# An encoder block on one core: TensorE's instructions held in the kernel's own order, the pieces of five stages and of the last gate rearranged

## The chip, the cores and the metric

The kernel runs on one core of a Trainium2 chip. The metric is the time of one execution of the whole program in device microseconds; the figure for the kernel before is the median of three runs. One further execution was recorded by the hardware profiler; all rows of the trace are of that one.

## What is computed

One layer of a bidirectional encoder, 256 tokens by 2048 features, all in float32:

```python
h = rms_norm(x, attn_norm)
qa, ka, va, qb, kb, vb, ga, gb = split(h @ w_in)
ya = windowed_gqa(qa, ka, va, ...)          # 8 heads, banded
yb = dilated_attention(qb, kb, vb, ...)     # 12 heads in 3 groups
merged = sigmoid(ga) * (ya @ w_branch_a) + sigmoid(gb) * (yb @ w_branch_b)
x = x + merged @ w_out
hf = rms_norm(x, ffn_norm)
g = dwconv_centred(hf @ w_ffn_gate, conv_w, conv_b)
x = x + (gelu(g) * (hf @ w_ffn_up)) @ w_ffn_down
gate_p = sigmoid(rms_norm(x, ple_norm) @ w_ple_gate)
x = x + gate_p * (p @ w_ple_proj)
return rms_norm(x, final_norm)
```

Nearly all of the work is the product of 256 rows with some 340 MB of weights, each of which is read once.

## The kernel before, in words

**Products in two halves.** A float32 operand is split into a high part that TensorE's fast float32 format holds exactly and a low rest. A product is then three fast matmuls: high by high, high by low, low by high (`thirds`, lines 466 to 468 for the high and low of both operands). For every weight block of 128x128 ScalarE makes the high part (L357, into `wh` or `vh`) and VectorE the low one (L358, into `wl` or `vl`). These go into a store of 56 blocks, 40 in the tiles `w*` and 16 in `v*`, which is used as a ring: `drop` gives blocks back when the kernel has written down their last matmul, and calls `pump`, which at once writes down the production of the next units as long as they fit (`produce`). So at each place of the program the weights of the next two pieces or so are written down already, and VectorE, which takes its instructions in one fixed order, has them ahead of what the kernel writes later.

**Pieces by eight and by seven.** The weight stream is cut into pieces. Within a stage that multiplies 128-token rows by two column groups of 512 (`quads`, `quad_stage`), a piece covers two chunks of 128 features. Kind "s" makes the 2x2 block product with eight `thirds`, which is 24 matmuls; kinds "Z" and "Y" make it after Winograd with seven, which is 21, from sums of the activations (`combos`, made by `combine` and `sums_of`) and sums of the weights. Part of the sums of the weights is made in DRAM by adding DMAs from GpSimd's queue (`sum_ahead`), part by VectorE in `sum_of_weights` (L336). A piece by seven puts 28 blocks through the store and a piece by eight 16. The strings `GATES`, `OUTS`, `DOWN` and `ALT` say piece by piece which kind it is.

**Stages.** In order of the program: A (projections and attention); for j = 0 to 3 a gate stage Bj, then `ba`j and `bb`j (the two branch products of kind "w", 24 matmuls a piece); D0 and D1 (the output projection, 8 pieces each); E0 (gate and up of the first half of the MLP: each `product` is 16 matmuls 128x512 and then 16 of 128x256, lines 409 and 416; the first four products run jointly); F00 and F01 (the down projection, 11 pieces each); E1, F10, F11 likewise for the second half; pp0 and pp1 (the projection of p, one "s" piece each); then the last gate: G0 (8 pieces, two column groups, kinds by `ALT`), G2 and G3 (4 pieces each, kind "w", one column group each); and the final norm.

**The end of a quad stage.** The seven sums lie in the PSUM banks M1, M7, M5, M6, M2, M3, M4, and the fourth result in P22; pieces by eight write M2, M3, M4 and P22 alone. In the last piece, which is by eight, `row_sums` first combines M1, M6, M7, M5 (L938 to L942) and then, after every second of its eight `thirds`, calls `end(t, n)` for row half t and column group n. In D and F this is `residual`'s `finish`: L1059 adds the bank to the residual rows `xr`, and for n = 1 L1061 adds the combined sums over all 1024 columns of that row half. `end(1, 1)` has slot 8: it is written down after the last `thirds`, after the blocks of the last piece were given back and after the units that then fit the store were written down.

**Turns.** The next product needs the new rows turned round: `turn_back` takes a pair of feature chunks and makes four TensorE transpositions (L987) in the order (chunk 0, half 0), (chunk 0, half 1), (chunk 1, half 0), (chunk 1, half 1) into one PSUM bank, which ScalarE and VectorE then read out (L571 and L572, or L990 and L991). `rows_pair` turns `xr` into `hf` (before E0) or `pl` (before the last gate), `merged_pair` turns the gated rows into `merged`. Where these stand in the program is set by `at((stage, piece, slot), ...)`: they are written down before that slot's `thirds`; in E0 the place is the chunk number k of the joint products, and 16 matmuls are written at a time.

**What sets the order on the engines.** The framework's scheduler takes the program and its own estimate of times and fixes the order of each engine's instructions: of those that it thinks ready it takes the one that stands first in the program. An instruction that would wait is overtaken, on TensorE too. Once fixed, each engine runs its list in order.

Of the kernel before, what the change touches and what calls it, by code (L numbers as in the profile page):

```python
# [20 lines left out]
D = 2048  # L21
KC = D // P
# [71 lines left out]
WIDE = 2 * T  # L94
_JOBS = _plan()
NA = len(_JOBS)
ALT = "ZsZsZsZs"
GATES = ("sssssYYs", "YsYYsYYs", "YsYYsYYs", "YsYYsYYs")
OUTS = "ZsZZsZZs"
DOWN = ("YYsYsYsYsYs", "ZsZZsZsZsZs")  # L100


def _ffn(half):
# [10 lines left out]
def _pieces():  # L114

    pieces, stages = [], {}

    def blocks(stage, items):
        stages[stage] = range(len(pieces), len(pieces) + len(items) // PIECE)
        for i in range(0, len(items), PIECE):  # L120
            pieces.append(("f", items[i:i + PIECE]))

    def quads(stage, n0, n1, pattern, k0=0):
        stages[stage] = range(len(pieces), len(pieces) + len(pattern))
        for i, c in enumerate(pattern):
            a, b = k0 + 2 * i, k0 + 2 * i + 1
            pieces.append((c, [(n1, a), (n1, b), (n0, a), (n0, b)] if c == "Z" else
                           [(n1, a), (n0, a), (n1, b), (n0, b)] if c == "Y" else
                           [(n0, a), (n1, a), (n1, b), (n0, b)]))

    def wide(stage, n, chunks):
        stages[stage] = range(len(pieces), len(pieces) + chunks // 4)
        for k in range(0, chunks, 4):
            pieces.append(("w", [(n, k + i) for i in range(4)]))

    a = [("w_in", k, j[2]) for k in range(KC) for j in _JOBS[:FIRST]]
    for _, _, n in _JOBS[FIRST:]:
        a += [("w_in", k, c) for k in range(KC) for c in (n if isinstance(n, tuple) else (n,))]
    blocks("A", a)
    for j in range(4):  # L140
        quads("B%d" % j, ("w_in", GA * P + j * WIDE), ("w_in", GB * P + j * WIDE), GATES[j])
        wide("ba%d" % j, ("w_branch_a", j * WIDE), QH)
        wide("bb%d" % j, ("w_branch_b", j * WIDE), HG)
    for s in range(2):
        quads("D%d" % s, ("w_out", 2 * s * WIDE), ("w_out", (2 * s + 1) * WIDE), OUTS)
    for half in range(2):
        names = {"g": "w_ffn_gate", "u": "w_ffn_up"}
        jobs = [(names[kind], f) for kind, f in _ffn(half)]
        joint = 0 if half else JOINT
        e = [(name, k, f) for k in range(KC) for name, f in jobs[:joint]]  # L150
        e += [(name, k, f) for name, f in jobs[joint:] for k in range(KC)]
        blocks("E%d" % half, e)
        for s in range(2):
            quads("F%d%d" % (half, s), ("w_ffn_down", 2 * s * WIDE), ("w_ffn_down", (2 * s + 1) * WIDE),
                  DOWN[half], half * FHALF)
    for s in range(2):
        stages["pp%d" % s] = [len(pieces)]
        n0, n1 = ("w_ple_proj", 2 * s * WIDE), ("w_ple_proj", (2 * s + 1) * WIDE)
        pieces.append(("s", [(n0, 0), (n1, 0), (n1, 1), (n0, 1)]))
    quads("G0", ("w_ple_gate", 0), ("w_ple_gate", WIDE), ALT)  # L160
    for s in (2, 3):
        wide("G%d" % s, ("w_ple_gate", s * WIDE), KC)
    return pieces, stages


# [31 lines left out]
def _encoder(ctx: ExitStack, tc, xt, pt, xrow, cols, gainrow, table, onehot, mask, ident_in, wts, out):  # L197
# [50 lines left out]

    made, taken, raws, left_of = {}, {}, {}, {}
    state = {"unit": 0, "at": 0, "early": True, "load": 0}  # L250
    store, free = {}, deque()
    rawt = wpool.tile([P, RAW * P], F32, name="raw")
    rawfree = deque(range(RAW))
    loads = []
# [2 lines left out]
    def extend(which, pool):  # L257

        store[which] = [pool.tile([P, STORE[which] * P], FR, name=which + half) for half in ("h", "l")]
        free.extend((which, b) for b in range(STORE[which]))  # L260

    extend("w", wpool)

# [116 lines left out]

    def drop(u, n=None):
        n = n or len(taken[u])
        free.extend(taken[u].popleft() for _ in range(n))
        made[u][1] += n
        if not taken[u]:
            del made[u], taken[u]
        pump()
# [82 lines left out]
    def part(m, t):  # L470
        return [m[:, c + t * P:c + (t + 1) * P] for c in (0, T)]

    def quad_stage(stage, moving, combos=None, tags=("M2", "M3", "M4", "P22")):
# [24 lines left out]
        for i, p in enumerate(pieces):  # L498
            kind = _PIECES[p][0]
            us = _UNITS_OF[p]  # L500
            if (stage, i) not in ends:
                a, b = moving(2 * i), moving(2 * i + 1)
            if kind == "s":
                final = i == len(pieces) - 1
                for g in range(8):
                    run_due(stage, i, g)
                    t, n, c = (g // 4, g // 2 % 2, g % 2) if final else (g // 2 % 2, g % 2, g // 4)
                    w = cut(us[c], n if c == 0 else 1 - n)
                    put(tags[2 * t + n], part((a, b)[c], t), w)
                    if not final and g % 4 == 3:  # L510
                        drop(us[c])
                if final:
                    drop(us[0])
                    drop(us[1])
            else:
                s = combos(i)
                sums = [(s[:, 0, e], s[:, 1, e]) for e in range(4)]
                m1, m2, m4 = (part(a, 0), part(b, 0), part(b, 1)) if (stage, i) not in ends else ends[stage, i]
                if kind == "Z":
                    todo = (("M6", sums[1], 0, 0), ("M3", sums[3], 0, 1), ("M1", m1, 1, 0), ("M2", m2, 1, 1),  # L520
                            ("M7", sums[2], 2, 0), ("M4", m4, 2, 1), ("M5", sums[0], 2, 2))
                else:
                    todo = (("M6", sums[1], 0, 0), ("M1", m1, 0, 1), ("M3", sums[3], 1, 0), ("M2", m2, 1, 1),
                            ("M7", sums[2], 2, 0), ("M5", sums[0], 2, 1), ("M4", m4, 2, 2))
                for g, (name, stationary, u, c) in enumerate(todo):
                    run_due(stage, i, g)
                    put(name, stationary, cut(us[u], c))
                    drop(us[u], 4)
# [84 lines left out]
    def spread_sums(pieces, slots):  # L613

        last = len(slots) - 10
        for e, p in enumerate(pieces):
            first = e * last // max(len(pieces) - 1, 1)
            for n, step in enumerate(sum_ahead(p)):
                at(slots[first + 3 * n], step)
# [3 lines left out]
    def at(i, f, *a):  # L623

        due.setdefault(i, []).append((f, a))
# [262 lines left out]
    def summed(*stages):  # L888
        return [p for stage in stages for p in _STAGES[stage] if _PIECES[p][0] in "ZY"]
# [62 lines left out]
    def quads(stage, moving, combos, finish):  # L952
        last = len(_STAGES[stage]) - 1
        row_sums(stage, last, finish)
        quad_stage(stage, moving, combos)
        run_due(stage, last, 8)
# [42 lines left out]
        turn_back(which, pair, held["merged"], lambda t: c[t][:, pair % 2 * T:(pair % 2 + 1) * T], None)  # L999

    def merged_turns(stage, j, c):
        for i, when in enumerate(((stage, 0, 3), (stage, 1, 1))):
            at(when, merged_pair, "P22", 2 * j + i, c)

    def halved(r):
# [14 lines left out]
    for n in range(2):  # L1020
        at(("bb3", 0, 4 * n), load_rows, n)

    for j in range(4):

        def gated(t, n, a):
# [3 lines left out]
            nc.scalar.activation(c, a, AF.Tanh, scale=rh[:, t:t + 1])  # L1029

        if j == 1:
            at(("ba1", 0, 0), combine, "merged", held["merged"], 0, 4)
        if j == 3:
            at(("B3", 2, 4), combine, "merged", held["merged"], 2, 0)
# [44 lines left out]
    held["ssq"] = sc.tile([P, 2, 2], F32, name="ssq", bufs=1)  # L1079
    residual("D0", 0, lambda k: held["merged"][:, k, :], "merged", True)  # L1080
    hf = big.tile([P, KC, 2 * T], FR, name="hf", tag="R0")
    for pair, when in enumerate((("D1", 0, 2), ("D1", 0, 5), ("D1", 1, 0), ("D1", 1, 3))):
        at(when, rows_pair, "P22", pair, hf, 1)
    residual("D1", 1, lambda k: held["merged"][:, k, :], "merged", True)
    for pair, which in enumerate(("M2", "M3", "M4", "P22")):
        at(("E0", 2 + pair), rows_pair, which, 4 + pair, hf, 1)

    def norm_columns():
        at(("E0", 13), spread, 1, diagonal(rows_root()))
# [100 lines left out]
    for half in range(2):  # L1190
# [7 lines left out]
        for (kind, n), a in zip(jobs, accs):  # L1198
            mlp(kind, n, a)
        turns["e"] = 5 if half else 2  # L1200
        spread_sums(summed("F10", "F11") if half else summed("F00", "F01", "G0"),
                    [(stage, i, 0) for i in range(1, len(jobs) - joint)])
        for i, (kind, n) in enumerate(jobs[joint:]):
            run_due(stage, i, 0)
# [15 lines left out]
    last = big.tile([P, 6 * 2 * WIDE], F32, name="last", tag="R1")  # L1220
    ph = last[:, :2 * D].rearrange("p (t c) -> p t c", t=2)
    gains = last[:, 2 * D:]
    at(("G0", 0, 0), lambda: keep(nc.sync.dma_start(gains, gainrow)))
    for pair, which in enumerate(("M2", "M3", "M4", "P22")):
        at(("pp0", 0, 4 + pair), rows_pair, which, 4 + pair, pl, 2)

# [1 line left out]
        held["rp"] = halved(rows_root())  # L1228

    at(("pp1", 0, 0), ple_root)  # L1230
    at(("pp1", 0, 4), combine, "pl", pl, 4, 2)
    at(("G0", 1, 4), combine, "pl", pl, 6, 3)
    names = ("M1", "M6", "M7", "M5")

    class Rows:
# [29 lines left out]
    def first_rows(t, n, a):  # L1265
        c = held["c"][t][:, cut[n]]
        nc.vector.tensor_tensor(c, a, c, op=ALU.add)
        ple(t, n, c, c)

    quads("G0", lambda k: pl[:, k, :], lambda i: combos["pl", i], first_rows)  # L1270
    c = outputs()
    for a, t in zip(wide_stage("G2", lambda k: pl[:, k, :], ("M1", "M7")), range(2)):
        ple(t, 2, a, c[t][:, cut[0]])
    accs = wide_stage("G3", lambda k: pl[:, k, :], ("M5", "M6"), 2)
    known = sc.tile([P, 2], F32, name="known", bufs=1)
    nc.vector.tensor_reduce(known, ssq[:, :, :3], axis=AX.X, op=ALU.add)
# [77 lines left out]
```

## Time and profile before

| what | value |
|---|---|
| median of three runs | 1452.42 us (1451.77 to 1452.98) |
| the profiled execution's own time | 1452.4 us |
| its span, first to last instruction | 1450.6 us |
| mean granted TensorE clock | 0.998 |
| VectorE, ScalarE busy | 1198.7 us (83%), 862.7 us (59%) |
| D0 begins, D1 begins, E0 begins | 539.19, 580.52, 624.08 us |
| F11 begins, pp0 begins | 1285.26, 1342.41 us |
| last matmul begins | 1440.65 us |

A row of the timeline reads: start, length, engine, line, operation, tiles written and read, shape, how many such instructions were merged into the row, and in brackets how long the engine stood idle before it and what released it. A matmul's length of 0.39 us holds its way through the array; the next one starts about 0.23 us after it, so the distance of starts is what one costs. "PE" is TensorE, "DVE" VectorE, "ACT" ScalarE, "POOL" GpSimd, "SP" SyncE.

### The profile page before, as it was taken

To read this page: it belongs to the slowest core of one execution; us is meant where nothing else is said; L and a number is where in the kernel's file an instruction comes from. 1 tells how busy PE (TensorE), PEld (TensorE's weight loads), DVE (VectorE), ACT (ScalarE), POOL (GpSimd) and SP (SyncE) were. 2 spreads that over 40 slices of the span, in tenths; PEclk is the share of its full clock that TensorE was granted. 3 is DMA by queue.
4 is the path that set the end of the run, shared out by engine and by line. 5 is a ranking of instruction groups with operands and counts; after the bars stand their busy time and mean duration, and the time that the engine had idled before them with its cause. 6 is when DMAs were issued, how large, how long until landed. Compare 5 with 4: busy or idle time off the path is not lost.

```text
span 1450.6 us, 20676 instructions
## 1 busy us (share of the span) xinstructions
PE 1438.4 (99%) x7449; PEld 1230.1 (85%) x7449; DVE 1198.7 (83%) x1758; ACT 862.7 (59%) x1271; POOL 111.7 (8%) x145
## 2 busy tenths in 40 slices
PE   9999999999999999999999999999999999999997
PEld 8888888888888888788888888888888888888886
DVE  7677665679999999988787789898877878899995
ACT  7555544546656566666566556565665655666763
POOL 0012121100000000001111100000111110000000
PEclk9999999999999999999999999999999999999999
DMA  9799999866578577577999966578898885758561
GB/s 323 261 314 243 238 255 288 224 193 216 195 231 264 183 260 258 187 271 223 265 258 262 265 191 202 166 252 259 250 244 250 261 248 174 246 194 281 181 237 59
DMA packets 113347, 339.88 MB, mean 234 GB/s; under 512 B 12564, under 2 KB 17556, under 8 KB 113116
## 3 DMA queue, kind: packets, MB, share of 16 engines
q1 hardware_dynamic: 94604, 301.72, 60.8%
q0 software_dynamic: 17920, 35.66, 15.3%
q8 instruction: 58, 0.95, 0.3%
q10 hardware_dynamic: 720, 1.19, 0.2%
q14 instruction: 45, 0.37, 0.1%
HBM read 336.38 MB, written 52.21 MB: 268 GB/s over the span
## 4 chain that ended last, share of the span: by engine, by line
PE 97%; DVE 1%; DMA 1%; ACT 1%; issue 0%; SPq 0%; POOLq 0%; POOL 0%; DVEq 0%; ACTq 0%
PE bank L409 29%; PE bank L416 15%; PE bank L466 14%; PE bank L467 14%; PE bank L468 14%; PE bank L455 2%; PE bank L457 2%; PE bank L456 2%; PE bank L393 2%; PE bank L394 1%; DMA raw<-in_wts 1%; PE bank L987 1%; PE bank L794 0%; PE bank L742 0%; PE bank L741 0%
## 5 line engine op out<-in xcount | busy, mean ns | idle before, releaser
L357 ACT ACTIVATE wh<-raw 128x1024 fp32r<-128x1024 f32 (+3 forms) x549 | 489.8, 912 | 313.3 <-PE bank L468 114.4
L358 DVE TENSOR_TENSOR wl<-raw,wh 128x1024 fp32r<-128x1024 f32 (+3 forms) x549 | 557.7, 1040 | 139.0 <-ACT wh L357 73.2
L409 PE MATMUL bank<-hf,wh 128*128 128x512 f32 x1008 | 245.3, 391 | 0.3 <-DVE c L942 0.3
L409 PEld LDWEIGHTS bank<-hf,wh 128*128 128x128 f32 x1008 | 185.4, 188 | 36.4 <-DVE c L942 0.5
L357 ACT ACTIVATE vh<-raw 128x1024 fp32r<-128x1024 f32 (+2 forms) x185 | 155.4, 853 | 78.5 <-PE bank L409 35.2
L358 DVE TENSOR_TENSOR vl<-raw,vh 128x1024 fp32r<-128x1024 f32 (+2 forms) x185 | 176.3, 968 | 29.4 <-issue 11.5
L314 POOL DMA_DIRECT2D ahead<-in_wts x110 | 92.4, 946 | 768.4 <-DMA ahead<-in_wts 740.1
L416 PEld LDWEIGHTS bank<-hf,wl 128*128 128x128 f32 x1008 | 131.2, 191 | 5.0
L416 PE MATMUL bank<-hf,wl 128*128 128x256 f32 x1008 | 135.3, 283 | 0.0
L555 ACT ACTIVATE t<-bank 128x256 f32<-128x256 f32 x122 | 46.4, 383 | 101.3 <-PE bank L416 95.6
L409 PE MATMUL bank<-hs,wh 128*128 128x512 f32 x432 | 103.6, 392 | 0.0
L409 PE MATMUL bank<-hf,vh 128*128 128x512 f32 x400 | 99.6, 391 | 0.2 <-DVE hf L572 0.2
L409 PEld LDWEIGHTS bank<-hs,wh 128*128 128x128 f32 x432 | 79.5, 188 | 15.6
L409 PEld LDWEIGHTS bank<-hf,vh 128*128 128x128 f32 x400 | 73.4, 188 | 14.8 <-DVE hf L572 0.7
L467 PE MATMUL bank<-wl,act 128*128 128x512 f32 x193 | 75.2, 390 | 0.0
L468 PE MATMUL bank<-wh,act 128*128 128x512 f32 x193 | 75.0, 390 | 0.0
L466 PE MATMUL bank<-wh,act 128*128 128x512 f32 x193 | 74.6, 391 | 0.0
L336 DVE TENSOR_TENSOR raw<-raw 128x512 f32<-128x512 f32 x87 | 57.1, 683 | 0.2
L416 PE MATMUL bank<-hs,wl 128*128 128x256 f32 x432 | 56.6, 284 | 0.0
L416 PE MATMUL bank<-hf,vl 128*128 128x256 f32 x400 | 56.0, 283 | 0.0
L416 PEld LDWEIGHTS bank<-hs,wl 128*128 128x128 f32 x432 | 54.5, 191 | 1.0
L416 PEld LDWEIGHTS bank<-hf,vl 128*128 128x128 f32 x400 | 53.1, 191 | 1.9
(283 smaller groups left out, 2567.4 us busy)
## 6 DMA issues: line engine op xcount, KB each, us to landing
raw<-in_wts SPq DMA_DIRECT2D x412, 512.0 KB, 5.9
raw<-in_wts SPq DMA_DIRECT2D x47, 768.0 KB, 6.1
ahead<-in_wts POOLq DMA_DIRECT2D x110, 256.0 KB, 8.2
raw<-ahead SPq DMA_DIRECT2D x81, 256.0 KB, 4.2
ahead<-in_wts SPq DMA_DIRECT2D x55, 256.0 KB, 8.1
ahead<-ahead POOLq DMA_DIRECT2D x26, 256.0 KB, 6.2
raw<-in_wts SPq DMA_DIRECT2D x9, 256.0 KB, 4.3
xr<-in_xrow SPq DMA_DIRECT2D x4, 512.0 KB, 6.7
```

The source lines that it names most:

```text
L314: keep(nc.sync.dma_start(dst, src) if op is None else nc.gpsimd.dma_start(dst, src, accum_op=op))
L336: nc.vector.tensor_tensor(q, three, q, op=op)
L357: nc.scalar.activation(hi, src, AF.Copy)
L358: nc.vector.tensor_tensor(lo, src, hi.bitcast(F32), op=ALU.subtract)
L393: nc.tensor.matmul(acc, hi, m, start=first, stop=False, skip_group_check=True)
L409: nc.tensor.matmul(acc, weights(u, o)[0], m, start=first, stop=False, skip_group_check=True)
L416: nc.tensor.matmul(acc[:, T:], weights(u, o)[1], m[:, :T], start=False, stop=last, skip_group_check=True)
L455: nc.tensor.matmul(acc[:, :n * P], xh, hi, start=(k == 0), stop=False)
L466: nc.tensor.matmul(acc, sh, wh, start=first, stop=False)
L467: nc.tensor.matmul(acc, sh, wl, start=False, stop=False)
L468: nc.tensor.matmul(acc, sl, wh, start=False, stop=last)
L555: keep(nc.scalar.activation(t, acc[:, T:], AF.Copy, scale=scale))
```

## The change

1. From the gate stage B1 on, TensorE's instructions keep the order in which the kernel writes them (`manual_schedule` for the engine PE). The other engines are ordered by the scheduler as before.
2. The stages B1, B2, B3, D0 and D1 take their pairs of chunks in the order 0, 2, 1, 3, 5, 4, 6, 7 (`ORDER`), and their kinds are permuted with them, so that they begin with two pieces by seven; which pairs are by seven stays the same. F10 and F11 begin with two pieces by seven too: pair 1 is now by seven in place of pair 2.
3. The turns move: `merged_pair` from slots 3 of piece 0 and 1 of piece 1 to slots 6 and 4; in D1 two pairs are left of four, at slot 6 of piece 0 and slot 3 of piece 1; in E0 there are six of eight, at chunks 0, 1, 2, 4, 5 and 8. Those of F11 (piece 0 slot 6, piece 1 slots 2 and 5, piece 2 slot 1) and of pp0 (slots 4 to 7) stay where they were.
4. The last gate runs G2 first, then G0, then G3. G0 has five pieces by seven and three by eight in place of four and four; the sums ahead of its last two are made in E1, and its sums of activations in pp1 and G2.
5. The 16 blocks of the store that come with the second pool join the ring behind block 39 of the first, not wherever the ring happens to stand.

```diff
-ALT = "ZsZsZsZs"
-GATES = ("sssssYYs", "YsYYsYYs", "YsYYsYYs", "YsYYsYYs")
-OUTS = "ZsZZsZZs"
-DOWN = ("YYsYsYsYsYs", "ZsZZsZsZsZs")
+ALT = "ZsZZsZZs"
+GATES = ("sssssYYs", "YYsYYsYs", "YYsYYsYs", "YYsYYsYs")
+OUTS = ("ZZsZZsZs", "ZZsZZsZs")
+DOWN = ("YYsYsYsYsYs", "ZZsZsZsZsZs")
+ORDER = {stage: (0, 2, 1, 3, 5, 4, 6, 7) for stage in ("B1", "B2", "B3", "D0", "D1")}
...
+    wide("G2", ("w_ple_gate", 2 * WIDE), KC)
     quads("G0", ("w_ple_gate", 0), ("w_ple_gate", WIDE), ALT)
-    for s in (2, 3):
-        wide("G%d" % s, ("w_ple_gate", s * WIDE), KC)
+    wide("G3", ("w_ple_gate", 3 * WIDE), KC)
...
-        free.extend((which, b) for b in range(STORE[which]))
+        (pending if taken else free).extend((which, b) for b in range(STORE[which]))
...
-        free.extend(taken[u].popleft() for _ in range(n))
+        for _ in range(n):
+            free.append(taken[u].popleft())
+            if free[-1] == ("w", STORE["w"] - 1):
+                free.extend(pending)
+                pending.clear()
...
-        for i, when in enumerate(((stage, 0, 3), (stage, 1, 1))):
+        for i, when in enumerate(((stage, 0, 6), (stage, 1, 4))):
             at(when, merged_pair, "P22", 2 * j + i, c)
...
+    in_order = lambda *engines: tc.manual_schedule(engines={getattr(mybir.EngineType, e) for e in engines})
+    ordered = ctx.enter_context(ExitStack())
...
         if j == 1:
+            ordered.enter_context(in_order("PE"))
...
-    for pair, when in enumerate((("D1", 0, 2), ("D1", 0, 5), ("D1", 1, 0), ("D1", 1, 3))):
+    for pair, when in enumerate((("D1", 0, 6), ("D1", 1, 3))):
         at(when, rows_pair, "P22", pair, hf, 1)
...
-    for pair, which in enumerate(("M2", "M3", "M4", "P22")):
-        at(("E0", 2 + pair), rows_pair, which, 4 + pair, hf, 1)
+    for pair, (k, which) in enumerate(((0, "M2"), (1, "M3"), (2, "M4"), (4, "P22"), (5, "M2"), (8, "M3"))):
+        at(("E0", k), rows_pair, which, 2 + pair, hf, 1)
...
-        spread_sums(summed("F10", "F11") if half else summed("F00", "F01", "G0"),
+        spread_sums(summed("F10", "F11") + summed("G0")[3:] if half else summed("F00", "F01") + summed("G0")[:3],
...
-    at(("G0", 0, 0), lambda: keep(nc.sync.dma_start(gains, gainrow)))
+    at(("G2", 0, 0), lambda: keep(nc.sync.dma_start(gains, gainrow)))
...
-    at(("pp1", 0, 4), combine, "pl", pl, 4, 2)
-    at(("G0", 1, 4), combine, "pl", pl, 6, 3)
+    at(("pp1", 0, 4), combine, "pl", pl, 3, 2)
+    at(("G2", 0, 2), combine, "pl", pl, 5, 3)
+    at(("G2", 1, 2), combine, "pl", pl, 6, 4)
...
+    c = outputs()
+    for a, t in zip(wide_stage("G2", lambda k: pl[:, k, :], ("M2", "M4")), range(2)):
+        ple(t, 2, a, c[t][:, cut[0]])
     quads("G0", lambda k: pl[:, k, :], lambda i: combos["pl", i], first_rows)
     c = outputs()
-    for a, t in zip(wide_stage("G2", lambda k: pl[:, k, :], ("M1", "M7")), range(2)):
-        ple(t, 2, a, c[t][:, cut[0]])
```

In `quad_stage` the numbers of the pair, of its chunks, sums and ends go through `ORDER`.

More of the change, by code (lines that the diff above doesn't have):

```diff
@@ L125, in quads @@
         for i, c in enumerate(pattern):
-            a, b = k0 + 2 * i, k0 + 2 * i + 1
+            pair = ORDER[stage][i] if stage in ORDER else i
+            a, b = k0 + 2 * pair, k0 + 2 * pair + 1
             pieces.append((c, [(n1, a), (n1, b), (n0, a), (n0, b)] if c == "Z" else
@@ L144, in _pieces @@
     for s in range(2):
-        quads("D%d" % s, ("w_out", 2 * s * WIDE), ("w_out", (2 * s + 1) * WIDE), OUTS)
+        quads("D%d" % s, ("w_out", 2 * s * WIDE), ("w_out", (2 * s + 1) * WIDE), OUTS[s])
     for half in range(2):
@@ L250, in _encoder @@
     state = {"unit": 0, "at": 0, "early": True, "load": 0}
-    store, free = {}, deque()
+    store, free, pending = {}, deque(), []
     rawt = wpool.tile([P, RAW * P], F32, name="raw")
@@ L500, in quad_stage @@
             us = _UNITS_OF[p]
-            if (stage, i) not in ends:
-                a, b = moving(2 * i), moving(2 * i + 1)
+            pair = ORDER[stage][i] if stage in ORDER else i
+            if (stage, pair) not in ends:
+                a, b = moving(2 * pair), moving(2 * pair + 1)
             if kind == "s":
@@ L515, in quad_stage @@
             else:
-                s = combos(i)
+                s = combos(pair)
                 sums = [(s[:, 0, e], s[:, 1, e]) for e in range(4)]
-                m1, m2, m4 = (part(a, 0), part(b, 0), part(b, 1)) if (stage, i) not in ends else ends[stage, i]
+                m1, m2, m4 = (part(a, 0), part(b, 0), part(b, 1)) if (stage, pair) not in ends else ends[stage, pair]
                 if kind == "Z":
```

## The prediction, made before any run of the change

> **What bounds the kernel now.** I read the page first: the busy time of each engine and the chain that ended last.
>
> ```profile
> span 1450.6 us, 20676 instructions
> PE 1438.4 (99%) x7449; PEld 1230.1 (85%) x7449; DVE 1198.7 (83%) x1758; ACT 862.7 (59%) x1271; POOL 111.7 (8%) x145
> PE 97%; DVE 1%; DMA 1%; ACT 1%; issue 0%; SPq 0%; POOLq 0%; POOL 0%; DVEq 0%; ACTq 0%
> ```
>
> TensorE is the bound in nearly the whole span. So I asked what TensorE waited for, and then the timeline of it at the longest wait, and the busy time in stretches where nothing is special.
>
> ```profile
> PE bank L237 <- DVE mhalf L232: 1.1, 1, 1.1
> PE bank L466 <- ACT wh L357: 0.9, 1, 0.9
> PE bank L409 <- DVE c L942: 0.3, 1, 0.3
> PE bank L409 <- DVE hf L572: 0.2, 1, 0.2
> ...
> 615.63 0.39 PE L467 MATMUL bank<-vl,S 128*128 128x512 f32 x1
> 616.92 0.50 PE L466 MATMUL bank<-wh,S 128*128 128x512 f32 x1 [0.90 <-ACT wh L357]
> ...
> 612.00:620.00 8.00, 7.10 (x31) 1.00 0.69 203
> 1357.00:1441.00 84.00, 84.00 (x371) 69.11 (x370) 69.19 (x106) 47.83 (x75) 2.54 (x2) 1.00 0.48 167
> ```
>
> There are four waits. The first lies before the first product and is untouched; the other three, 0.9 + 0.3 + 0.2 = 1.4 us, lie at the end of D1 and in E0. The row from 612 to 620 shows what the longest costs: TensorE busy 7.10 of 8.00 us, at a granted clock of 1.00. In the stretch of the last gate (last row: TensorE busy 84.00 of 84.00, VectorE 69.19) there is none. A kernel in that state can gain by fewer matmuls and by those 1.4 us, and can lose at every place where TensorE is made to wait.
>
> **Part 1, fewer matmuls.** G0 gets one piece by seven in place of one by eight: 21 matmuls for 24. The price of one is the distance of starts; in this row from E0 it is (2.88 - 0.39) / 11 = 0.226 us.
>
> ```profile
> 624.08 2.88 PE L409 MATMUL bank<-hf,wh 128*128 128x512 f32 x12
> ```
>
> Three of them are 0.7 us. VectorE pays for it with 12 more blocks (three L358 of 0.68 us, rows below), two more weight sums (1.28 us by L336) and one more set of activation sums, which I estimate at as much as the sums and halves above, together some 5 us; GpSimd's and SyncE's queues get four more transfers in E1. I cost that at nothing on the path: VectorE has 84.00 - 69.19 = 14.8 us free in the last gate. If that cover were gone it would cost TensorE up to those 5 us at G0's end.
>
> **Part 2, the waits that are there.** From 615.63 to 616.92 are 1.29 us where 0.23 would do, so 1.06 us are lost, and 0.3 + 0.2 us in E0. D1 now has two turns fewer to read out and no longer ends with two pieces by seven in a row, so VectorE is less behind there. I take all of it as gone: 1.6 us. With part 1 the gain is 2.3 us, and I see no more than about 1 us beyond it (restarts around these waits).
>
> **Part 3, the held order.** This is where I differ from the optimistic reading. In the list before, TensorE overtakes transpositions whose rows aren't ready. I looked up where it does, against the place that the kernel writes. At the start of pp0 and at the end of VectorE's work for F11:
>
> ```profile
> 1342.41 0.39 PE L466 MATMUL bank<-vh,t 128*128 128x512 f32 x1
> ...
> 1345.19 0.27 PE L987 MATMUL bank<-ident,xr 128*128 128x128 f32 x1
> 1345.22 0.48 PE L466 MATMUL bank<-vh,t 128*128 128x512 f32 x1
> ...
> 1349.23 1.04 PE L987 MATMUL bank<-ident,xr 128*128 128x128 f32 x8
> ...
> 1344.95 0.68 DVE L358 TENSOR_TENSOR vl<-raw,vh 128x512 fp32r<-128x512 f32 x1
> 1345.55 1.28 DVE L336 TENSOR_TENSOR raw<-raw 128x512 f32<-128x512 f32 x2
> 1346.75 0.68 DVE L1059 TENSOR_TENSOR xr<-xr,bank 128x512 f32<-128x512 f32 x1
> 1347.46 1.23 DVE L1061 TENSOR_TENSOR xr<-xr,c 128x1024 f32<-128x1024 f32 x1
> ```
>
> The kernel writes the four transpositions of pair 4 at slot 4, four `thirds` or 2.8 us into the stage. One is executed there, at 1345.19: it turns half 0. The next one turns half 1, whose rows are finished by the L1061 that ends at 1347.46 + 1.23 = 1348.69, 6.3 us into the stage; TensorE does products in the meantime and the rest of the transpositions at 1349.23. Held in order it stands still from about 1345.3 to 1348.7: **3.4 us**. Behind the waiting transposition is queued everything on TensorE. Nothing on VectorE's side is moved out of the way: F11's end is as before, and the two units of weights written down ahead of `end(1, 1)` are now two of G2, 16 blocks, where they were 8 blocks and two sums (L358 and L336 above); 2.4 us either way. If the scheduler put those two behind the residual, the wait would shrink to 1.0 us; that is the lower end.
>
> The same at the start of F11, whose first turn has slot 6 of piece 0 before and after:
>
> ```profile
> 1285.26 0.39 PE L466 MATMUL bank<-wh,S 128*128 128x512 f32 x1
> ...
> 1290.48 0.27 PE L987 MATMUL bank<-ident,xr 128*128 128x128 f32 x1
> ...
> 1292.44 0.49 PE L987 MATMUL bank<-ident,xr 128*128 128x128 f32 x3
> ...
> 1287.29 2.35 DVE L358 TENSOR_TENSOR wl<-raw,wh 128x1024 fp32r<-128x1024 f32 x2
> 1289.56 0.68 DVE L1059 TENSOR_TENSOR xr<-xr,bank 128x512 f32<-128x512 f32 x1
> 1290.16 0.68 DVE L358 TENSOR_TENSOR wl<-raw,wh 128x512 fp32r<-128x512 f32 x1
> 1290.76 1.22 DVE L1061 TENSOR_TENSOR xr<-xr,c 128x1024 f32<-128x1024 f32 x1
> ```
>
> Six `thirds` are 18 x 0.226 = 4.1 us, so TensorE comes to the first transposition at 1289.3 and to the second at 1289.5. The first wants the bank P22, which L1059 leaves at 1290.24; the second wants the rows of L1061, ready at 1291.98. The wait is **2.5 us**; nothing if both L358 groups came behind the residual, 3.8 us if the sums of the second piece by seven (1.28 us) came ahead of it.
>
> At the start of D1 the first turn moves from slot 2 to slot 6:
>
> ```profile
> 580.52 0.39 PE L466 MATMUL bank<-vh,S 128*128 128x512 f32 x1
> ...
> 586.67 0.27 PE L987 MATMUL bank<-ident,xr 128*128 128x128 f32 x1
> ...
> 586.81 1.21 DVE L1061 TENSOR_TENSOR xr<-xr,c 128x1024 f32<-128x1024 f32 x1
> ```
>
> TensorE comes to the second transposition at 580.52 + 4.1 + 0.1 = 584.7 and the rows come at 588.02: 3.3 us by this row. D0 now ends with a piece by eight, one by seven and one by eight, as F10 does, so I take F10's lag, 6.7 us into the stage for D0's 7.5: **2.5 us**, between 0 and 3.3. A wait for bank M3 at its second `thirds` (some 0.4 us) is swallowed by this later one.
>
> In E0 pair 4 is the first one that needs D1's last rows. It is written after pair 2, 16 matmuls and pair 3:
>
> ```profile
> 628.92 1.22 DVE L1061 TENSOR_TENSOR xr<-xr,c 128x1024 f32<-128x1024 f32 x1
> ...
> 634.13 1.21 DVE L1061 TENSOR_TENSOR xr<-xr,c 128x1024 f32<-128x1024 f32 x1
> 635.77 1.47 PE L987 MATMUL bank<-ident,xr 128*128 128x128 f32 x12
> ```
>
> From the last row a transposition costs (1.47 - 0.27) / 11 = 0.11 us. So TensorE is there 0.44 + 16 x 0.226 + 0.44 + 0.11 = 4.6 us into E0, and before, the rows of half 1 came at 635.34, 11.3 us into it. D1's end is now relieved, so I take F11's lag of 6.3 us: **1.7 us**, between 0 and 6.6.
>
> Sum of the four: 3.4 + 2.5 + 2.5 + 1.7 = 10.1 us.
>
> **Part 4, what I cost at nothing.** The turns of `merged` at slots 6 and 4: their rows were ready about 3 to 4 us into the stage and TensorE comes after 4.1; the second weight sums now written ahead of them could make that up to 1 us late in each of four stages, kept for the range. The later turns of F11 follow each other by three `thirds`, 2.0 us, and the bank must be read out in between by two reads each of ScalarE and VectorE; 0 to 1.5 us in all, kept for the range. G2 ahead of G0 changes no count, and G3's banks M5 and M6 are free unless G0's last sums come late. The ring of the store joined whole saves VectorE some splits and TensorE nothing.
>
> **The forecast.** The profiled execution took 1452.4 us, 1.8 us around its span, and the median of the runs is 1452.42, so the sum needs no correction: 1452.4 - 0.7 - 1.6 + 10.1 = 1460.2 us. A measurement of this kernel can tell about 0.2%, 2.9 us, from no change.
>
> **Rivals.**
>
> Other side: VectorE clears the residual in time. The scheduler works out VectorE's list anew against a TensorE that waits, and could take L1059 and L1061 ahead of the weights. It decides at one point: whether L1061 of half 1 ends within 4.2 us of the start of D1 and F11, 4.6 of E0 and 2.8 of pp0. Then only the gain is left, 2.3 to 3.3 us: 1449.1 to 1450.1 us. For it: VectorE is busy 83%, not 100%, and has the production ahead of need. Against: at all four places the L358 rows stand ahead of the last L1059 by their place in the program, which the change leaves.
>
> Half of it: D1, E0 and F11 come out even, since their places were moved or their pieces permuted, and pp0 alone waits: 1452.4 - 2.3 + 3.4 = 1453.5 us. For it: pp0 is the only place with neither a moved turn nor other pieces ahead. Against: F11's first turn hasn't moved either.
>
> The order isn't really held, and the scheduler still overtakes: then only part 1 counts, 1451.7 us. Against it: the diff opens the context before stage B1's products and closes it at the end.
>
> The clock falls after the waits. In the one long wait of the trace, 1.06 us, the granted clock stays at 1.00 (the row from 612 to 620 above). A wait of 3.4 us at pp0 is outside what the trace shows. If half the clock were granted for as long again as such a wait, each of the two to four waits would cost 1.7 us more, and with all four the time would be 1467 us. [...]
>
> **How the numbers follow.** Waits at most of the four places, 1460.2 us with its own range of 1454 to 1465: 0.62. The clock falls as well: 0.05. VectorE in time: 0.20, of which 0.14 gains over 2.9 us and 0.06 less. pp0 alone: 0.10, 0.07 of it within 2.9 us. Order not held: 0.03. So faster 0.14, same 0.06 + 0.07 + 0.03 = 0.16, slower 0.62 + 0.05 + 0.03 = 0.70. The range runs from 1449.5, which takes in half of the case without waits, to 1465, where E0 waits its full 6.6 us; what lies outside is some 0.1 below and 0.1 above.
>
> **What would show it.** In the waits of TensorE, the transposition line must be the first entry, released by VectorE's L1061 (its line number a little higher), four times, 1.7 to 3.4 us each, at slot 6 of D1 and F11, in E0's first products and at slot 4 of pp0; transpositions come in groups of whole fours. The wait for ACT's `wh` in D1 is gone. TensorE has 3 matmuls fewer. G3 begins without a wait. I am wrong if the waits of TensorE stay under 3 us in all, or if the waits are there and the time still falls, which would mean that the order before cost more than its gaps show.

## The result, and the profile after

| | before | after |
|---|---|---|
| median of five runs | 1452.42 us (1451.77 to 1452.98) | 1486.24 us (1485.14 to 1487.05) |
| ratio, 95% interval | | 1.0231 [1.0217, 1.0245] |
| profiled execution, its span | 1452.4, 1450.6 us | 1486.96, 1485.2 us |
| mean granted TensorE clock | 0.998 | 0.990 |
| last matmul begins | 1440.65 us | 1474.82 us |

The change costs 33.8 us, 2.3%. In the kernel after, the transposition is L996, a weight's high part is made by L361 and its low part by L362, the residual is L1072 and L1074, and the read-out of a turn is L580 and L581, or L1000 for `merged`. The page of the profile after:

```profile
span 1485.2 us, 20588 instructions
PE 1448.0 (97%) x7446; PEld 1236.6 (83%) x7446; DVE 1202.7 (81%) x1718; ACT 859.4 (58%) x1224; POOL 113.3 (8%) x148
PE 86%; DVE 9%; issue 2%; ACT 1%; DMA 1%; SPq 0%; POOLq 0%; POOL 0%; DVEq 0%; ACTq 0%
```

TensorE has the three matmuls fewer, and VectorE now holds 9% of the chain that ended last, where it held 1%. The waits of TensorE (total, times, longest):

```profile
PE bank L996 <- DVE xr L1074: 9.1, 4, 3.2
PE bank L996 <- DVE pl L581: 3.3, 2, 1.7
PE bank L996 <- DVE merged L1000: 3.0, 3, 1.3
PE bank L996 <- DVE xr L1072: 2.6, 2, 1.5
PE bank L996 <- DVE c L1060: 2.0, 1, 2.0
PE bank L996 <- DVE hf L581: 1.7, 1, 1.7
```

All waits together are 27.4 us, against 2.5 before. The first line is the one that was forecast: transpositions that wait for the last residual rows, four times, longest 3.2. Of the lines below it only `c` L1060 is rows again. In the others the transpositions want the PSUM bank P22, and it has not been emptied: L1072 adds the last result of the stage before, which lies in P22, to `xr`, and `pl`, `hf` and `merged` are the read-out of the turn before. The timeline at the start of F11 shows rows and bank, on TensorE, VectorE and ScalarE:

```profile
1307.06 0.33 PE L996 MATMUL bank<-ident,xr 128*128 128x128 f32 x1 [1.54 <-DVE xr L1072]
1310.47 0.90 PE L996 MATMUL bank<-ident,xr 128*128 128x128 f32 x3 [3.08 <-DVE xr L1074]
...
1312.02 0.63 PE L476 MATMUL bank<-wh,S 128*128 128x512 f32 x1
1312.45 0.63 PE L474 MATMUL bank<-wh,S 128*128 128x512 f32 x1
...
1316.82 1.09 PE L996 MATMUL bank<-ident,xr 128*128 128x128 f32 x4 [1.61 <-DVE pl L581]
```

```profile
1306.33 0.68 DVE L1072 TENSOR_TENSOR xr<-xr,bank 128x512 f32<-128x512 f32 x1
1306.92 1.22 DVE L362 TENSOR_TENSOR wl<-raw,wh 128x1024 fp32r<-128x1024 f32 x1
1308.06 1.22 DVE L362 TENSOR_TENSOR vl<-raw,vh 128x1024 fp32r<-128x1024 f32 x1
1309.19 1.22 DVE L1074 TENSOR_TENSOR xr<-xr,c 128x1024 f32<-128x1024 f32 x1
1310.33 2.35 DVE L362 TENSOR_TENSOR wl<-raw,wh 128x1024 fp32r<-128x1024 f32 x2
1312.60 0.47 DVE L581 SCALAR_TENSOR_TENSOR pl<-bank,cl,pl 128x256 fp32r<-128x256 f32 x1
1315.05 1.22 DVE L362 TENSOR_TENSOR wl<-raw,wh 128x1024 fp32r<-128x1024 f32 x1 [1.98 <-ACT wh L361]
1316.20 0.48 DVE L581 SCALAR_TENSOR_TENSOR pl<-bank,cl,pl 128x256 fp32r<-128x256 f32 x1
```

```profile
1313.97 1.06 ACT L361 ACTIVATE wh<-raw 128x1024 fp32r<-128x1024 f32 x1 [2.01 <-PE bank L476]
```

Read them as a loop. TensorE stands until L1074 ends at 1310.41. It gives blocks of the store back late, and ScalarE waits 2.01 us for L476 before it can make the next high part; VectorE waits 1.98 us for that high part; and the second read-out of the first turn, L581 at 1316.20, stands behind that weight in VectorE's fixed list. The next turn waits for this read-out, another 1.61 us. So a late row can make a second wait; whether the read-out would have been early without it, this trace doesn't show. And the two matmuls at 1312.02 and 1312.45 are 0.43 us apart, not 0.23. The busy time in stretches says why (columns: length; busy time and count of TensorE, its weight loads, VectorE, ScalarE, GpSimd; granted clock; DMA share; GB/s):

```profile
374.30:377.70 3.40, 3.40 (x9) 2.62 (x9) 3.40 (x4) 1.06 (x1) 0.00 (x0) 0.50 0.96 367
596.10:599.50 3.40, 3.40 (x10) 2.35 (x8) 3.40 (x5) 1.31 (x2) 0.00 (x0) 0.50 0.70 201
601.50:605.00 3.50, 3.50 (x18) 2.95 (x19) 2.86 (x5) 2.92 (x5) 0.00 (x0) 1.00 0.60 197
1309.50:1319.70 10.20, 7.62 (x21) 5.87 (x22) 7.64 (x11) 4.39 (x8) 0.00 (x0) 0.50 0.63 201
1377.80:1384.60 6.80, 6.10 (x20) 5.06 (x21) 3.34 (x9) 3.78 (x8) 0.71 (x1) 0.50 0.19 67
```

In four stretches, 23.9 us in all, half the clock is granted. They lie behind the waits: 1.97 us in B1, 1.03 and 1.41 close together in D1, 1.54 and 3.08 in F11, 3.15 in pp0. By the distances of starts in them (0.43 for 0.23 us, about 0.2 for 0.11 in transpositions) I count some 9 us lost.

So the last matmul's 34.2 us are, roughly, 24.9 of added waits and 9 of half clock, less 0.7 for three matmuls. Which of these hang together, only runs can say.

### The profile page after: what moved, and what is told of

It reads as the page before. It is cut to its first block, busy times and chain, and to the rows that moved or that the text cites. A ratio compares the mean times of both kernels' runs of the same rounds, so it can differ in the third digit from the quotient of the medians.

```text
span 1485.2 us, 20588 instructions
## 1 busy us (share of the span) xinstructions
PE 1448.0 (97%) x7446; PEld 1236.6 (83%) x7446; DVE 1202.7 (81%) x1718; ACT 859.4 (58%) x1224; POOL 113.3 (8%) x148
## 4 chain that ended last, share of the span: by engine, by line
PE 86%; DVE 9%; issue 2%; ACT 1%; DMA 1%; SPq 0%; POOLq 0%; POOL 0%; DVEq 0%; ACTq 0%
PE bank L417 28%; PE bank L424 15%; PE bank L474 11%; PE bank L475 11%; PE bank L476 11%; DVE wl L362 3%; PE bank L463 2%; PE bank L465 2%; PE bank L464 2%; PE bank L401 2%; DVE vl L362 1%; PE bank L402 1%; DMA raw<-in_wts 1%; DVE xr L1074 1%; PE bank L996 1%
## 5 line engine op out<-in xcount | busy, mean ns | idle before, releaser
L361 ACT ACTIVATE wh<-raw 128x1024 fp32r<-128x1024 f32 (+3 forms) x498 | 486.4, 991 | 351.3 <-PE bank L417 122.4
L362 DVE TENSOR_TENSOR wl<-raw,wh 128x1024 fp32r<-128x1024 f32 (+3 forms) x498 | 556.7, 1138 | 161.0 <-ACT wh L361 81.4
L362 DVE TENSOR_TENSOR vl<-raw,vh 128x512 fp32r<-128x512 f32 (+2 forms) x188 | 174.9, 946 | 35.2 <-ACT vh L361 14.2
L361 ACT ACTIVATE vh<-raw 128x512 fp32r<-128x512 f32 (+2 forms) x188 | 154.4, 835 | 69.3 <-PE bank L476 30.6
L476 PE MATMUL bank<-wh,act 128*128 128x512 f32 x194 | 75.5, 389 | 0.0
```

Of the source, the lines that this page charges most:

```text
L361: nc.scalar.activation(hi, src, AF.Copy)
L362: nc.vector.tensor_tensor(lo, src, hi.bitcast(F32), op=ALU.subtract)
L476: nc.tensor.matmul(acc, sl, wh, start=False, stop=last)
```

## The experiments

Theory: the held order makes nearly all of it, as rows that come late, and the half clock comes with it. Rivals: the other parts of the change cost time of their own; or what TensorE waits for is the read-out and VectorE's list, so that curing the rows only moves the wait. "Before" and "after" in the edits say which kernel was changed.

**The change without the held order.** After, with one line less:

```diff
-            ordered.enter_context(in_order("PE"))
```

> The changed kernel with TensorE's order left to the scheduler again; everything else of the change stays. Theory (the held order makes the turns' transpositions wait for VectorE, and the long waits halve the clock): the 25.6 us of waits and the 7 us of half clock go, TensorE's waits are under 4 us and the mean granted clock is back at 0.998; 1450 to 1454 us. Rival (the rearranged pieces, the last gate or the ring cost the time themselves, by VectorE's load): the time stays above 1470 us, with the waits turned into waits for weights.

Measured 1458.42 us, ratio to before 1.0039 [1.0024, 1.0054]. Its waits:

```profile
PE bank L474 <- DVE c L1057: 1.8, 1, 1.8
PE bank L475 <- DVE wl L362: 1.8, 3, 1.0
...
PE bank L996 <- DVE c L1059: 0.9, 1, 0.9
PE bank L417 <- DVE c L951: 0.6, 1, 0.6
```

The line of L1074 is gone and the mean clock is 0.998 again. The held order is worth 27.8 of the 33.8 us in this kernel. But 6.0 us remain, more than the theory allowed.

**The held order without the rest.** Before, with the context opened at the same place; F10 and F11 begin with two pieces by seven as in the change:

```diff
         if j == 1:
+            ctx.enter_context(tc.manual_schedule(engines={mybir.EngineType.PE}))
```

> The kernel before with TensorE's order held from B1 on and nothing else, except that F10 and F11 begin with two pieces by seven, as in the change, since F11's four turns need the bank P22 before the first piece by eight. Theory: the order alone costs at least as much as the whole change, since the turns stand earlier (slot 3 in B, slot 2 in D1) and wait longer: 1478 to 1500 us. Rival (the rearrangement is the larger part of the loss): only the 8 to 10 us of the prediction's four places, 1460 to 1463 us.

Measured 1509.15 us, 1.0382 [1.0365, 1.0399]. Its waits begin:

```profile
PE bank L987 <- DVE xr L1062: 9.9, 4, 3.3
PE bank L466 <- DVE merged L991: 7.1, 4, 2.5
PE bank L987 <- DVE xr L1060: 5.2, 2, 3.7
PE bank L987 <- DVE c L1048: 4.8, 5, 1.8
```

The same kinds of wait, and more of them: +56.7 us. The rest of the change takes 22.9 us out of a cost that the held order makes. By their places these are the moved turns and pieces, but the last gate and the ring differ between the two kernels too, and no run separates them under the held order. This rest is a cure for something that the kernel before did not have.

**The held order where there are no turns.** Before, held from F00 to the end of F10 only:

```diff
+        if not half:
+            held_pe = ExitStack()
+            held_pe.enter_context(tc.manual_schedule(engines={mybir.EngineType.PE}))
         residual("F%d0" % half, 0, activation_row, "act", half)
+        if half:
+            held_pe.close()
```

> The kernel before with TensorE's order held only from F00 to F10, some 410 us in which no rows are turned. Theory (the held order costs where turns wait): 1452 to 1456 us, waits of at most 3 us there. Rival (the held order costs everywhere, because the scheduler orders VectorE's list worse against it): a share of the 57 us of the order alone by length, 1465 us or more.

Measured 1455.81 us, 1.0023 [1.0013, 1.0032]: +3.4 us over some 400 us of held program, in small waits for weights. By length that would be some 9 us over the 1080 us from B1 on, an estimate, against the 56.7 us of the run above. So most of the price is at the turns.

**The residual first.** After, with the last residual written ahead of the units that then fit the store:

```diff
                 if final:
+                    run_due(stage, i, 8)
                     drop(us[0])
```

> The changed kernel with the call of end(1, 1) written before the last piece's blocks are given back, so that VectorE has L1059 and L1061 of the last quarter ahead of the 16 blocks of weights that then become possible. Theory (the rows come late because VectorE takes its list in the program's order): at D1, E0, F11 and pp0 the rows come 1.1 to 2.4 us earlier, the waits for them fall from 11.7 us to 3 to 7 us and part of the half clock goes with them: 1472 to 1480 us. Rival (VectorE has too much work in those places, whatever the order): the waits turn into waits for weights, 1484 to 1488 us.

Measured 1485.59 us, 1.0227 [1.0212, 1.0242], no better. Its waits (all lines one number higher):

```profile
PE bank L997 <- DVE pl L582: 7.6, 2, 5.8
PE bank L997 <- DVE hf L582: 5.7, 1, 5.7
PE bank L997 <- DVE xr L1075: 2.9, 3, 1.9
```

The rows come in time (9.1 us of waits fell to 2.9), and the read-outs take their place (3.3 and 1.7 rose to 7.6 and 5.7). The theory of late rows alone fails here; of the half clock only 3.4 us go, 20.5 are left of 23.9. The rival's time was right, but it named waits for weights. Most of the new waits are for the bank; those for weights grew too, by 1.7 us between 948 and 952 us.

**Rows that are never late.** After, with each transposition fed from a constant tile; the turned activations, and so the output, are no longer the encoder's:

```diff
-                nc.tensor.transpose(p[:, k, t * P:(t + 1) * P], src(t)[:, k * P:(k + 1) * P], ident)
+                nc.tensor.transpose(p[:, k, t * P:(t + 1) * P], ident, ident)
```

> The changed kernel with every turn made of a constant tile in place of the new rows: the same transpositions, banks and read-outs, but no transposition waits for VectorE's rows any more (so merged, hf and pl hold other numbers, and the output is not the encoder's). It takes away the wait for the rows alone. Theory of one cause (the rows): the waits of the transpositions nearly all go, and with them the half clock, 1458 to 1463 us. Theory of a chain (one PSUM bank and VectorE's list stand behind the rows): pp0, E0 and B1 no longer wait, but in D1 and F11 the second turn waits for the first one's read-out, as it did when the residual was put first, 1468 to 1479 us.

Measured 1479.73 us, 1.0187 [1.017, 1.0204]. The waits, and VectorE at the start of F11:

```profile
PE bank L996 <- DVE pl L581: 6.5, 2, 5.0
PE bank L996 <- DVE merged L1000: 5.0, 4, 2.2
PE bank L996 <- DVE hf L581: 4.9, 1, 4.9
PE bank L996 <- DVE xr L1072: 2.6, 2, 1.6
```

```profile
1309.77 1.22 DVE L1074 TENSOR_TENSOR xr<-xr,c 128x1024 f32<-128x1024 f32 x1
1310.90 2.35 DVE L362 TENSOR_TENSOR wl<-raw,wh 128x1024 fp32r<-128x1024 f32 x2
1313.17 0.47 DVE L581 SCALAR_TENSOR_TENSOR pl<-bank,cl,pl 128x256 fp32r<-128x256 f32 x1
1313.57 1.21 DVE L362 TENSOR_TENSOR wl<-raw,wh 128x1024 fp32r<-128x1024 f32 x1
1314.70 0.47 DVE L581 SCALAR_TENSOR_TENSOR pl<-bank,cl,pl 128x256 fp32r<-128x256 f32 x1
```

No transposition waits for rows any more (L1072 is here the release of the bank P22), and the kernel gains only 6.5 us of 33.8. The read-outs L581 stand behind L1074 and three weights in VectorE's list, so the second turn waits until 1315.2 whatever the first one's rows did. Counted from the start of L1074 that read-out ends after 5.4 us here and after 7.5 us in the kernel after: the loop by way of the store is worth 2.1 us of it. In D1 late rows make no difference to the read-outs at all. Counted in the same way, the first begins after 5.67 us here and after 5.68 in the kernel after, and both times it stands behind 4.62 us of weights (L362). The theory of one cause falls; what holds is a chain: one bank, a list on VectorE that can't be left, and a TensorE that may no longer do something else meanwhile. The time came out just above the range that went with the chain, and B1 does still wait, 2.18 us for the read-out of its first turn. Whether read-outs placed ahead of the weights would help, or only make weights late, was not tried.

**The turns of pp0 one stage later.** After, with

```diff
-        at(("pp0", 0, 4 + pair), rows_pair, which, 4 + pair, pl, 2)
+        at(("pp1", 0, pair), rows_pair, which, 4 + pair, pl, 2)
```

> The changed kernel with pp0's four turns written before pp1's first four slots in place of pp0's last four, 5.5 to 6 us after F11's end and not 2.8. Theory (the wait is for the rows, and the clock falls because of it): the wait of 3.15 us shrinks to 0.5 us or less and the 6.8 us of half clock there go: 1480 to 1483 us. Rival (the wait moves on, to the read-out of the turned rows or to G2's start): 1485 to 1487 us.

Measured 1480.61 us, 1.0196 [1.0181, 1.0212]: 5.6 us less than after. The wait there fell from 3.15 to 0.38 us and the granted clock behind it is 1.00. Here each turn has its own bank (M2, M3, M4, P22), so nothing takes the place of the wait. The wait is 2.8 us shorter, and by starts the half clock behind it had cost about 3 us. How the 5.6 us divide isn't clean: in F11 half clock lasts 6.83 us in this trace and not 10.24, which is another 1.4 us by starts.

**Busy instead of idle.** After, with dummy matmuls written ahead of the four turns that wait longest:

```diff
+        for _ in range(fill):
+            nc.tensor.matmul(p[:, 1, T - P:], ones, ones, start=True, stop=True)
```

> The changed kernel with small matmuls of a constant by itself put in front of four of the waiting turns (9 before the first turn of B1, 7 in D1, 14 in F11, 15 in pp0, about 0.21 us each), so that TensorE works where it stood still; their results are overwritten by the transpositions. Theory (a long wait halves the clock for one or more stretches of 3.4 us): the waits become as much work, the half clock goes in three or four of the places, mean clock at least 0.996, 1478 to 1482 us. Rival (the halved clock costs nothing or has another cause): 1485 to 1488 us or more, by the added matmuls.

Measured 1483.63 us, 1.0211 [1.0196, 1.0226]. The half clock is left in two stretches:

```profile
600.80:604.20 3.40, 3.40 (x11) 2.73 (x9) 2.73 (x6) 2.30 (x4) 0.00 (x0) 0.50 0.54 168
1317.60:1321.00 3.40, 3.40 (x12) 2.72 (x11) 3.01 (x5) 1.92 (x4) 0.00 (x0) 0.50 0.66 202
```

That is 6.8 us in place of 23.9, and the median gains 2.6 us: a small gain, though the slowest run here, 1483.94 us, is below the fastest of the kernel after, 1485.14. The clock has a price of its own. By starts 6.5 us of loss are gone; that less comes out is due in part to the read-outs again (3.3 us for `hf` at the place of 1.7), and the two stretches lie behind such waits.

**The remaining 6 us.** Three parts of the change alone, each on the kernel before: the last gate (G2, G0 with five pieces by seven, G3), the ring of the store, the turns of D1 and E0. And after without the held order, with the old pieces and `merged` turns, which leaves these three together. The edits are those of the change's diff, the ring's and the turns' core being:

```diff
-        free.extend((which, b) for b in range(STORE[which]))
+        (pending if taken else free).extend((which, b) for b in range(STORE[which]))
```

```diff
-    for pair, when in enumerate((("D1", 0, 2), ("D1", 0, 5), ("D1", 1, 0), ("D1", 1, 3))):
+    for pair, when in enumerate((("D1", 0, 6), ("D1", 1, 3))):
...
-    for pair, which in enumerate(("M2", "M3", "M4", "P22")):
+    for pair, (k, which) in enumerate(((0, "M2"), (1, "M3"), (2, "M4"), (4, "P22"), (5, "M2"), (8, "M3"))):
```

> The kernel before with the last gate of the change alone: G2 first, five pieces by seven in G0, their sums and the read of the gains moved with them. Three matmuls fewer and nothing late: 1450.5 to 1452.5 us by the prediction's part 1. Rival (VectorE is late for G3, or the two sums moved to E1 come late): 1455 us or more, with a wait for weights or for M5 in the last gate.

> The kernel before with the store's ring joined whole, alone. VectorE and ScalarE have fewer, longer instructions. Theory (the 3.7 us that the last gate, the ring and D1's and E0's turns lose together come from the turns, where the profile showed a transposition that waited 1.8 us for its rows at the start of E0): 1451.5 to 1453.5 us. Rival (the ring shifts the scheduler's list for VectorE, and weights come late): 1455 to 1457 us.

> The kernel before with two of D1's four turns moved to E0 and E0's six at the change's places, alone, in the scheduler's order. Theory: the turns in E0 wait for rows that VectorE has not finished, 1454.5 to 1457 us, with the wait of 0.9 us for weights in D1 gone. Rival (the relief of VectorE in D1 is the larger effect, and the ring costs the 3.7 us): 1450 to 1452 us.

> The changed kernel without the held order and with the old pieces: GATES, OUTS and DOWN as before, no ORDER, merged's turns back at slots 3 and 1. What is left of the change is the last gate, the joined ring, D1's two turns less and E0's six. Theory (the 6 us that the free order still loses come from beginning stages with two pieces by seven): 1449.5 to 1452 us, and TensorE's waits for weights in B2 and F11 are gone. Rival (they come from the last gate or the ring): 1456 to 1459 us.

| kernel | median | ratio to before |
|---|---|---|
| last gate alone | 1452.61 us | 1.0001 [0.9993, 1.001] |
| ring alone | 1456.06 us | 1.0026 [1.0016, 1.0036] |
| turns of D1 and E0 alone | 1454.06 us | 1.001 [1.0001, 1.0019] |
| these three, order free | 1456.27 us | 1.0025 [1.0017, 1.0034] |
| and the pieces (first experiment) | 1458.42 us | 1.0039 [1.0024, 1.0054] |

The last gate is no difference that can be measured. The theory that the pieces make the 6 us falls, and the ring is the largest part, as its rival said. It costs 3.6 us although it does what it is for, as its page and its waits show:

```profile
PE 1439.1 (99%) x7449; PEld 1228.9 (84%) x7449; DVE 1194.7 (82%) x1709; ACT 856.8 (59%) x1222; POOL 111.3 (8%) x145
```

```profile
PE bank L470 <- ACT wh L357: 2.4, 2, 2.0
...
PE bank L471 <- DVE wl L358: 0.8, 1, 0.8
```

VectorE has 49 instructions and 4.0 us of busy time fewer, and TensorE still waits longer for weights, most of it 2.02 us in D1: VectorE is off the bound here (82% busy, TensorE 99%), its saving was worth nothing, and the order that comes out is worse there. Why the order is worse stays open. The turns of D1 and E0 do take away the wait for `wh` in D1 and put another at E0's first turn, with the half clock behind it:

```profile
625.16 1.11 PE L987 MATMUL bank<-ident,xr 128*128 128x128 f32 x4 [2.26 <-DVE xr L1059]
```

The pieces that begin two by seven, with the later turns of `merged`, would be the difference of the last two rows of the table, about 2 us; the two intervals overlap, so this part is not shown. No version was faster than the kernel before. What was not tried is the held order with every turn put late, on a bank of its own.

## Why the prediction failed

The direction was right, the size was not: +7.8 us were forecast and +33.8 measured, 21 us above the range.

- **Part 1** was right in its count (7446 for 7449) and too small to be seen: the last gate alone gives 1.0001 [0.9993, 1.001] where the 0.7 us would be 0.9995.
- **Part 2**: the wait of 0.9 us for `wh` in D1 is gone, as forecast, by the moved turns. What takes its place is larger.
- **Part 3** was right in its mechanism and near in its sum. It forecast 10.1 us at four places, and the line of L1074 has 9.1 us at those four. But my terms ran from TensorE's arrival at the turn, and in F11 and D1 its first transposition already waits, 1.54 and 1.03 us for the bank. Counted so it is 11.7 us: pp0 3.15 for 3.4, F11 4.62 for 2.5, D1 2.44 for 2.5, E0 1.48 for 1.7. F11 is above the upper end of 3.8 that I kept for it: two L362, 2.3 us, came between L1072 and L1074, where one L358 of 0.68 us had stood.
- **Part 4, "what I cost at nothing", is the step that failed.** "The bank must be read out in between ... 0 to 1.5 us in all" for F11: measured 3.3 + 0.9 us for `pl`, and 1.7 for `hf` in D1, which I hadn't asked about. "Up to 1 us late in each of four stages" for the turns of `merged`: 2.0 us for `c` in B1, and 3.0 us in three stages for the read-out, not for the rows. Together these are 10.9 us of waits; I put nothing for them into the sum and at most 5.5 into the range. I priced the read-out by its own length against the 2.0 us between two turns. It stands in VectorE's fixed list instead, behind up to 4.62 us of weights in D1, and a TensorE held in order waits for it. For the most part this isn't a consequence of the late rows: with constant rows, where none is late, 27 of the 33.8 us remain.
- **The clock rival** (0.05, 1467 us) came true in kind, with some 9 us by starts. Behind the 0.05 stood one wait of 1.06 us at full clock; no run had shown what 3.4 us would do. Waits of 1.97 us in B1 and, with the turns of D1 and E0 alone, of 2.26 us in E0 were enough. With the range ending at 1465, it was both too unlikely and too cheap: I priced half clock for as long as the wait, 1.7 us a wait, and it came for 3.4, 6.8 and 10.2 us.
- **Other edits** were costed at nothing and cost some 6 us without the held order: the ring ("TensorE nothing") 3.6, the turns of D1 and E0 1.6, the pieces perhaps 2, not quite additive.
- The signs that I named held for the first entry of the waits, its four places and G3 without a wait. Their size held at two places; D1 and E0, 1.41 and 1.48 us, are below the 1.7 that I gave. None of the signs could have shown the size to be wrong, since all were about the rows.

## What to carry to other kernels

Before an engine that sets the time is held to program order, list each place where it now overtakes, and price there not only the first operand that comes late but the bank, the read-out and the buffers that its own standing still holds back. Ask of a cure what stands behind the instruction that it brings forward: on a chain through one bank and one fixed list, it moves the wait to the next link. And price idle time of TensorE at more than its length: here stretches of half clock of 3.41 to 10.24 us lay behind the waits.

## What the runs showed of the hardware

The granted clock of TensorE fell to 0.50 behind waits shorter than the 3.4 us that I had priced, and then for 3.41 us or two or three times that (6.83, 10.24 in the kernel after). Both waits of over 3 us in the kernel after, 3.08 and 3.15, had it. Waits of about 2 us did or did not. The 2.26 us in E0 with the new turns did, as that kernel's next stretch shows:

```profile
625.20:628.60 3.40, 3.40 (x10) 2.85 (x11) 3.40 (x6) 0.47 (x1) 0.00 (x0) 0.50 1.01 407
```

With the joined ring, 2.02 us in D1, which end at 618.57, did not:

```profile
616.00:618.50 2.50, 0.55 (x3) 0.12 (x1) 2.12 (x3) 1.26 (x3) 0.00 (x0) 1.00 0.39 111
618.50:620.00 1.50, 1.02 (x4) 0.54 (x4) 1.30 (x2) 1.50 (x3) 0.00 (x0) 1.00 0.85 311
620.00:622.00 2.00, 2.00 (x9) 1.66 (x10) 2.00 (x2) 0.90 (x2) 0.00 (x0) 1.00 0.89 324
```

Nor did 2.18 us in B1 with constant rows; and the wait in B1 for `c`, 1.97 us and half clock in the kernel after, is 1.95 us and full clock in the one with the residual first. Single waits of 1.28, 1.48 and 1.66 us in the kernel after left the clock at 1.00. So the length alone does not decide it in these traces, and what else does is not shown.

In B1 of the kernel after the clock did not fall at once: the wait ends at 372.82 us, and the stretch up to 374.25 still has 1.00, where the one from 374.30 has 0.50:

```profile
370.84:374.25 3.41, 1.44 (x9) 1.26 (x9) 3.41 (x4) 2.02 (x3) 0.00 (x0) 1.00 0.28 72
```
